# Seven block products for the first feed-forward product, an earlier second compression, and low parts on VectorE

## The chip, the cores and the metric

The kernel runs on one core of a Trainium2 chip. The metric is the device time of one launch in microseconds (us), lower is better. One profiled execution of the kernel before, with its trace, is what the prediction is made from.

## The reference, cut to what matters

One inference step of a decoder layer for 512 prompt tokens and 64 sample tokens (8 sequences of 8), which share the weights. Input projection, a sparse attention with a compressed, a selected and a window branch, a gated mixer, an output projection, and a feed-forward block:

```python
kc = compress_blocks(kv_full[:, :, 0], ...)   # keys
vc = compress_blocks(kv_full[:, :, 1], ...)   # values
h = x + jnp.concatenate([o_a, o_b], axis=-1) @ w_out
f = jax.nn.relu(rmsnorm(h, ln2_g) @ w_ff1)    # 1024 -> 4096
y = rmsnorm(h + (f * f) @ w_ff2, ln_f_g)      # 4096 -> 1024
```

## The kernel before, in words

Every large product is made in split form: an operand is cut into a high part (rounded copy, made by ScalarE) and a low part (the rest, a subtraction, mostly on VectorE), by `split` (L105). A product is then three matmuls: high with high, high with low, low with high. A weight tile of 128 rows by 512 columns is loaded into a `raw` tile and split into a unit `wu` of two halves by `load_unit` (L134).

The kernel is written in a tile framework: the author names pools of slots, the framework places every wait and, by a simulated timeline, the order of each engine's queue, with what is traced first going first among what is ready. Tiles of one tag in a pool share its slots (`bufs`).

**Sample attention** (L756 to L929) goes over four pairs of sequences. For a pair, `hidden` (L781) makes 32 matmuls `pcs` into a slot of the two-slot PSUM pool `psaA` and a `gelu` on ScalarE and VectorE; `compress_keys` (L791) follows it with a product `pk` in a slot of the same pool, `compress_values` (L798) with `pv`. Before, the tracing order for the first pair is keys' hidden, `pk`, the softmax (`soft`, L809), then values' hidden, `pv`. In `soft`, VectorE scales 1,032 columns of P and GpSimd 512 (L874).

**Output projection** (L942 to L1007). The mixer output `OTp` is split into `Hh` and `Hl` in eight pieces, the low parts on GpSimd (L995), the sample rows into `Hst`. 16 weight units `us` lie in the slots `fw` (3 + 5) and `fw2` (6 + 2). Ten groups of matmuls, one for a token tile t (four of 128 rows, t = 4 the 64 sample rows) and a column half, go in the order of L1003, sample rows last; a finished t is normed and transposed into Hh, Hl (L148).

**Feed-forward** (L1042 to L1099): eight chunks c of 512 hidden columns. `up` (L1047) makes, for each of four blocks m of 128 columns and each half of the 576 tokens (288), 24 matmuls: 192 in a chunk. `square` (L1054) makes relu, square and split into Fh, Fl; GpSimd copies the sample rows into Fst. `down` (L1072) makes ten groups: eight (t < 4) of 12 matmuls of 512 columns and two (t = 4) of 8, 112 in a chunk. `acc` (L966) adds a group onto the residual R: VectorE for t < 4; for t = 4 ScalarE copies half of it to `atmp`, VectorE adds into `atm2`, GpSimd adds onto R. `atmp` and `atm2` are tags of the pool `evp`, two slots each. PSUM for all groups are six banks taken in a fixed cycle from pools of 3, 2 and 1 (L957).

In the last chunk each t is followed by `last_norm` (L1015): ScalarE squares R into a tile `y` (tag `y`, two slots) with a row sum, VectorE and GpSimd make the factor, VectorE writes `y`, SyncE stores it. The last t (t = 3) has tiles of its own, two halves `yh`.

Of the kernel before, what the change touches and what calls it, by code (L numbers as in the profile page):

```python
# [90 lines left out]
def _body(ctx, tc, nc, I, O):  # L91
# [664 lines left out]
    with cs as c3:  # L756
# [34 lines left out]
        def compress_keys(pr, KW):  # L791
            gel = hidden(pr, 0)
            pk = psaA.tile([128, 512], F32, name="pk2", tag="acc")
# [4 lines left out]
        def compress_values(pr):  # L798
            gel = hidden(pr, 1)
            pv = psaA.tile([64, 2, 2, 64], F32, name="pv2", tag="acc")  # L800
            for sq in range(2):
                for h in range(2):
                    f = sq == 0 and h == 0
                    mm(pv[:, sq, h, :], gel[:, (h * 2 + sq) * 64:(h * 2 + sq) * 64 + 64], w2z[:, 1, 64:128],
                       f, True, f)
            dve.tensor_tensor(VB[pr][0:64].rearrange("p s (h d) -> p (s h) d", h=2),
                              pv.rearrange("p s h d -> p (s h) d"), bcast(b2r[0:64, 1], [[0, 4], [1, 64]]), op=ALU.add)
# [106 lines left out]
                        dst = OTs[gp * 64:gp * 64 + 64, h * 2 + a, c0:c0 + 16].rearrange("p (s q) -> p s q", s=2)  # L914
                        cpy("D" if h else "A", dst, ov[h * 64:h * 64 + 64, :, h, a, gp, :])

        compress_keys(0, W[0])
        prev = None
        for pr in range(4):
            P = soft(pr, W[0])  # L920
            compress_values(pr)
            if prev:
                values(*prev)
            prev = (pr, P, W[1])
            if pr < 3:
# [71 lines left out]
    split(Hst[:, :, 0:64], Hst[:, :, 64:128], OTs)  # L997
    for t in range(5):
        sp.dma_start(R[t], xin[t])
    with ExitStack() as c3:  # L1000
        n2 = c3.enter_context(tc.tile_pool(name="n2b", bufs=2, reuse_waits="tile"))
        done = set()
        for t, nh in ((0, 0), (1, 0), (2, 0), (3, 0), (0, 1), (1, 1), (2, 1), (3, 1), (4, 0), (4, 1)):  # L1003
# [7 lines left out]
    KC = 4  # L1011
    yo = [O["yp"].rearrange("b s d -> (b s) d")[t * 128:(t + 1) * 128] for t in range(4)]
    yo.append(O["ys"].rearrange("b s d -> (b s) d"))

    def last_norm(t, final):  # L1015
        rows = tsz[t]
        if final:

            y = [rp.tile([128, 512], F32, name="yh", tag=f"yh{h}", bufs=1) for h in range(2)]
            q = rp.tile([128, 512], F32, name="yq", tag="yq", bufs=1)  # L1020
            s2 = rp.tile([128, 2], F32, name="ss2", tag="ss2", bufs=1)
            ss = rp.tile([128, 1], F32, name="ssf", tag="ssf")
            for h in range(2):
                x = R[t][:, h * 512:h * 512 + 512]
                act.activation(q[:rows], x, AF.Square, accum_out=s2[:rows, h:h + 1])
                (dve if h else pool).tensor_tensor(y[h][:rows], x, gf[:rows, h * 512:h * 512 + 512], op=ALU.mult)
            dve.tensor_tensor(ss[:rows], s2[:rows, 0:1], s2[:rows, 1:2], op=ALU.add)
# [12 lines left out]

    w_ff1, w_ff2 = I["w_ff1"][0], I["w_ff2"][0]
    for c in range(32 // KC):  # L1042
        us = [load_unit(fw[k], w_ff1[k * 128:(k + 1) * 128, c * 512:c * 512 + 512], 512) for k in range(8)]
        Fh = fp.tile([128, KC, NT], F32R, name="Fh", tag="Fh")
        Fl = fp.tile([128, KC, NT], F32R, name="Fl", tag="Fl")
        Fst = fp.tile([128, KC, 128], F32R, name="Fst", tag="Fst")
# [5 lines left out]
                    mm(p[:, :288], w, a[:, k, c0:c0 + 288], k == 0 and j == 0, k == 7 and j == 2)  # L1052

        def square(m, pab):  # L1054
            r = rp.tile([128, NT], F32, name="relu", tag="relu")
            f2 = rp.tile([128, NT], F32, name="f2", tag="f2")
            for i, p in enumerate(pab):
                act.activation(r[:, i * 288:i * 288 + 288], p[:, :288], AF.Relu)  # L1058
            dve.tensor_tensor(f2, r, r, op=ALU.mult)  # L1059
            split(Fh[:, m], Fl[:, m], f2)  # L1060
            pool.tensor_copy(Fst[:, m, 0:64], Fh[:, m, 512:576].bitcast(F32))  # L1061
            pool.tensor_copy(Fst[:, m, 64:128], Fl[:, m, 512:576].bitcast(F32))

        for m0 in range(0, KC, 2):
# [7 lines left out]
        def down(t, nh, vs):  # L1072
            p = bank()
# [9 lines left out]
            acc(t, p, nh * 512, evp)  # L1083

        def down_units(nh):
            return [load_unit(fw2[nh * KC + m], w_ff2[(c * KC + m) * 128:(c * KC + m + 1) * 128, nh * 512:nh * 512 + 512], 512)
                    for m in range(KC)]

        if c < 32 // KC - 1:
# [76 lines left out]
```

## Time and profile before

| what | value |
|---|---|
| median of 3 runs | 828.01 us (827.09 to 829.6) |
| the profiled execution's own time | 827.65 us |
| its span, first to last instruction | 825.9 us |
| TensorE busy with matmuls | 789.6 us of the span |
| VectorE, ScalarE, GpSimd busy | 442.7, 353.4, 176.7 us |
| mean granted TensorE clock | 0.987 |

A row of the timeline has the start in us from the span's start, the duration, engine, line, operation, output<-inputs, shapes, a count where like instructions are merged, and in brackets the idle time of the engine just before and what ended it. PE is TensorE's matmul side, PEld its weight loads, DVE VectorE, ACT ScalarE, POOL GpSimd, SP SyncE's queue of transfers. Matmuls are pipelined, so the distance between starts is the pace, not the duration of one.

### The profile page before, as it was taken

How to read it: one execution, taken by the hardware profiler on the slowest of the kernel's cores; microseconds unless marked ns; L12 is line 12 of the kernel's file. 1: busy time of each engine (PE TensorE's matmuls, PEld its weight loads, DVE VectorE, ACT ScalarE, POOL GpSimd, SP SyncE). 2: the span in 40 equal slices, each digit the busy share in tenths (PEclk: the TensorE clock that was granted, in tenths of full speed). 3: DMA queues.
4: the chain of work that ended last, by engine and by line, in shares of the span. 5: the costliest groups of instructions: out<-in, count | busy, mean ns of one | idle time of the engine just before them, and what ended most of it. 6: DMA issues, size and time to landing. Idle time of an engine off the chain costs nothing.

```text
span 825.9 us, 13167 instructions
## 1 busy us (share of the span) xinstructions
PE 789.6 (96%) x4825; PEld 685.8 (83%) x4825; DVE 442.7 (54%) x980; ACT 353.4 (43%) x864; POOL 176.7 (21%) x219
## 2 busy tenths in 40 slices
PE   6989999999997998999989999999999999999996
PEld 5879888878675776778888998989989899898985
DVE  5345878888962347443756345163452634435325
ACT  6535478787842243432634232232322324232213
POOL 1103744454310116010211111111111111111112
PEclk9999999999997999999999999999999999999999
DMA  9771422000967545533324132041320413303003
GB/s 317 201 207 30 135 54 52 2 2 27 327 234 264 194 118 195 194 120 115 121 85 150 54 102 75 29 153 52 102 88 16 154 52 102 102 15 100 2 1 115
DMA packets 55187, 92.05 MB, mean 111 GB/s; under 512 B 7858, under 2 KB 19090, under 8 KB 54994
## 3 DMA queue, kind: packets, MB, share of 16 engines
q1 hardware_dynamic: 54866, 91.14, 34.8%
q8 instruction: 38, 0.62, 0.3%
q14 instruction: 27, 0.22, 0.1%
q0 software_dynamic: 256, 0.07, 0.0%
HBM read 86.92 MB, written 8.39 MB: 115 GB/s over the span
## 4 chain that ended last, share of the span: by engine, by line
PE 83%; DVE 7%; DMA 3%; ACT 3%; issue 2%; POOL 1%; POOLq 0%; SPq 0%; DVEq 0%; ACTq 0%
PE acc L95 52%; PE pcs L95 6%; PE pd L95 5%; PE o L95 4%; PE pu L95 3%; PE pq L95 3%; PE s L95 2%; PE tp L692 2%; DMA raw<-in_w_in 2%; DVE wu L107 1%; PE pc L95 1%; POOL wu L107 1%; DVE Q L522 1%; POOL rstd L145 1%; DMA raw<-in_w_ff 1%
## 5 line engine op out<-in xcount | busy, mean ns | idle before, releaser
L95 PE MATMUL acc<-Hh,wu 128*128 128x288 f32 x1024 | 204.9, 295 | 0.2 <-ACT Hh L106 0.2
L106 ACT ACTIVATE wu<-raw 128x512 fp32r<-128x512 f32 (+1 forms) x184 | 105.5, 614 | 152.6 <-PE acc L95 119.5
L95 PEld LDWEIGHTS acc<-Hh,wu 128*128 128x128 f32 x1024 | 164.3, 188 | 0.7 <-ACT Hh L106 0.4
L95 PE MATMUL acc<-wu,Fh 128*128 128x512 f32 x512 | 155.5, 389 | 0.0
L95 PE MATMUL acc<-Hl,wu 128*128 128x288 f32 x512 | 150.7, 295 | 0.0
L107 DVE TENSOR_TENSOR wu<-raw,wu 128x512 fp32r<-128x512 f32 x160 | 105.2, 695 | 47.2 <-ACT wu L106 47.2
L95 PEld LDWEIGHTS acc<-wu,Fh 128*128 128x128 f32 x512 | 95.7, 188 | 19.5
L95 PE MATMUL acc<-wu,Fl 128*128 128x512 f32 x256 | 97.1, 389 | 0.0
L95 PEld LDWEIGHTS acc<-Hl,wu 128*128 128x128 f32 x512 | 96.0, 188 | 0.3
L1059 DVE TENSOR_TENSOR f<-relu 128x576 f32<-128x576 f32 x32 | 24.2, 756 | 117.9 <-ACT relu L1058 117.9
L968 DVE TENSOR_TENSOR OTp<-acc,OTp 128x512 f32<-128x512 f32 x72 | 47.7, 687 | 62.4 <-PE acc L95 62.4
L1058 ACT ACTIVATE relu<-acc 128x288 f32<-128x288 f32 x64 | 26.2, 409 | 116.9 <-PE acc L95 116.9
L974 POOL TENSOR_TENSOR R<-atm,R 64x512 f32<-64x512 f32 x18 | 30.5, 1700 | 155.1 <-DVE atm L973 155.1
L95 PE MATMUL pd<-wu,AH 128*128 128x512 f32 (+1 forms) x192 | 55.2, 371 | 8.7 <-ACT wu L106 8.2
L95 PE MATMUL pcs<-G,w 128*128 128x256 f32 x256 | 61.5, 396 | 0.0
L1061 POOL CAST Fst<-Fh 128x64 fp32r<-128x64 f32 x32 | 23.5, 734 | 175.2 <-ACT Fh L106 118.7
L95 PEld LDWEIGHTS pcs<-G,w 128*128 128x128 f32 x256 | 49.7, 199 | 10.5 <-issue 3.6
L95 PEld LDWEIGHTS acc<-wu,Fl 128*128 128x128 f32 x256 | 48.1, 188 | 10.0
L95 PEld LDWEIGHTS pd<-wu,AH 128*128 128x128 f32 x192 | 34.7, 193 | 14.8 <-ACT wu L106 8.6
L668 ACT ACTIVATE P<-s,nm 128x32 f32<-128x32 f32 (+4 forms) x88 | 40.5, 464 | 14.5 <-DVE nm L667 14.0
L95 PE MATMUL acc<-wu,Hh 128*128 128x512 f32 x128 | 40.6, 397 | 0.0
L107 POOL TENSOR_TENSOR wu<-raw,wu 128x512 fp32r<-128x512 f32 (+1 forms) x24 | 30.8, 1301 | 44.2 <-ACT wu L106 44.2
(329 smaller groups left out, 1349.5 us busy)
## 6 DMA issues: line engine op xcount, KB each, us to landing
raw<-in_w_ff SPq DMA_DIRECT2D x128, 256.0 KB
G<-in_cache_kv SPq DMA_DIRECT2D x64, 256.0 KB
raw<-in_w_in SPq DMA_DIRECT2D x32, 256.0 KB
raw<-in_w_out SPq DMA_DIRECT2D x16, 256.0 KB
out_wins<-in_state_win_kv SPq DMA_DIRECT2D x8, 504.0 KB
xt<-in_x_t SPq DMA_DIRECT2D x8, 288.0 KB
x<-in_x_prompt SPq DMA_DIRECT2D x4, 512.0 KB
KW<-in_win_kt SPq DMA_DIRECT2D x4, 512.0 KB
```

The source lines that it names most:

```text
L95: pe.matmul(out, lhsT, rhs, start=start, stop=stop, skip_group_check=not first_in_bank)
L106: act.activation(hi, src, AF.Copy)
L107: eng.tensor_tensor(lo, src, hi.bitcast(F32), op=ALU.subtract)
L145: pool.tensor_tensor(r[:rows], ms[:rows], mhalf[:rows], op=ALU.pow)
L522: dve.tensor_tensor(Q[b, h, c0:c1], src, Q[a, h, c0:c1].bitcast(F32), op=ALU.subtract)
L668: act.activation(p_[:, c0:c0 + w], src, AF.Exp, bias=nm[:, br, g:g + 1], accum_out=l[:, br, g:g + 1])
L692: pe.transpose(t_[:w, g * 128:(g + 1) * 128], P[g][:, c0:c0 + w], ident)
L968: dve.tensor_tensor(R[t][:, c0:c0 + 512], p, R[t][:, c0:c0 + 512], op=ALU.add)
L974: pool.tensor_tensor(R[4][:, c0:c0 + 512], tm2, R[4][:, c0:c0 + 512], op=ALU.add)
L1058: act.activation(r[:, i * 288:i * 288 + 288], p[:, :288], AF.Relu)
L1059: dve.tensor_tensor(f2, r, r, op=ALU.mult)
L1061: pool.tensor_copy(Fst[:, m, 0:64], Fh[:, m, 512:576].bitcast(F32))
```

## The change

1. Sample attention: the first pair's two `hidden` are traced together ahead of the first `pk`; the gelu pool gets a second slot, and this first `pk` lies in the bank of `psm`.
2. The low parts of L995 go to VectorE.
3. From chunk 1 on, `up` is replaced by `seven(m0)` for each pair of blocks: the pair's product (1024 rows by 256 columns, by 576 tokens) is taken as 2 x 2 blocks of 512 rows, 128 columns and 288 tokens, and made of seven block products of 12 matmuls in place of eight. Sums of token blocks (`token_sums`, once, in chunk 0) and of weight blocks (`weight_sums`, for each pair) are made and split; the results are combined by five VectorE additions.
4. To make room: `y` has one slot, which the last t uses too; `evp` has one slot for each tag, and the weight sum `s3` and the last `yq` share the tag `atmp`; `raw` has 6 slots, `fw2` 4 + 2, the units go round two rings, `Hst` and `g2` lie in the norm pool, and sample rows come fifth in the output projection.
5. The last t's second half of `down` is made in two pieces of 256 columns.

```diff
-        ga_ = lpool("agel", 1)
+        ga_ = lpool("agel", 2)
...
-        compress_keys(0, W[0])
+        gel = [hidden(0, st) for st in range(2)]
+        compress_keys(0, W[0], gel[0], psm)
...
-            compress_values(pr)
+            compress_values(pr, gel[1] if pr == 0 else None)
...
-    pools['wraw'] = tpool("wraw2", 7)
-    evp = tpool("evp", 2)
+    pools['wraw'] = tpool("wraw2", 6)
+    evp = tpool("evp", 1)
...
-    fw2a = tpool("fw2a", 6)
-    fw2 = [fw2a] * 6 + [fw2b] * 2
+    fw2a = tpool("fw2a", 4)
+    fw2 = [fw2a] * 4 + [fw2b] * 2
...
+    ring, ring2 = itertools.cycle(fw), itertools.cycle(fw2)
...
-        split(Hh[:, k, 0:512], Hl[:, k, 0:512], OTp[:, k], pool)
-    us.append(out_units(1, fw2))
+        split(Hh[:, k, 0:512], Hl[:, k, 0:512], OTp[:, k])
+    us.append(out_units(1, fw2 + fw[:2]))
...
+    def token_sums(k):
...
+        def sub2(b, a):
+            x, y = tmp("tx"), tmp("ty")
+            dve.tensor_tensor(x, q(Hh, *b), q(Hh, *a), op=ALU.subtract)
+            dve.tensor_tensor(y, q(Hl, *b), q(Hl, *a), op=ALU.subtract)
+            dve.tensor_tensor(x, x, y, op=ALU.add)
+            return x
+        def sub1(b, x):
+            z = tmp("tz")
+            dve.tensor_tensor(z, q(Hh, *b), x, op=ALU.subtract)
+            dve.tensor_tensor(z, z, q(Hl, *b), op=ALU.add)
+            return z
+        t1 = sub2((0, 1), (0, 0))
+        split(T[0][0][:, k], T[0][1][:, k], t1)
+        t2 = sub1((1, 1), t1)
+        split(T[1][0][:, k], T[1][1][:, k], t2)
+        t4 = sub1((1, 0), t2)
+        split(T[2][0][:, k], T[2][1][:, k], t4)
+        t3 = sub2((1, 1), (0, 1))
+        split(Hh[:, k, N2:NT], Hl[:, k, N2:NT], t3)
+    def weight_sums(m0):
+        for i in range(2):
+            r = rp.tile([128, 4, 256], F32, name="fraw", tag=f"fraw{i}", bufs=1)
...
+        us = [next(ring).tile([128, 2, 512], F32R, name="wu", tag="w") for i in range(7)]
...
+        s3 = evp.tile([128, 512], F32, name="s3", tag="atmp").rearrange("p (k m) -> p k m", k=4)
+        put(0, a11)
+        dve.tensor_tensor(s3, a11, a21, op=ALU.subtract)
+        dve.tensor_tensor(a21, a21, a22, op=ALU.add)
+        dve.tensor_tensor(a11, a21, a11, op=ALU.subtract)
+        put(1, a11)
+        put(2, s3)
+        put(3, a21)
+        put(4, a12)
+        dve.tensor_tensor(a12, a12, a11, op=ALU.subtract)
+        put(5, a22)
+        put(6, a12)
+        return us
...
+            y = rp.tile([128, D], F32, name="y", tag="y", bufs=1)
...
-        y = rp.tile([128, D], F32, name="y", tag="y")
+        y = rp.tile([128, D], F32, name="y", tag="y", bufs=1)
...
+            prod(a, 0, half(H, 0, 0))
+            p1 = fs("p1")
+            act.activation(p1, a, AF.Copy)
+            prod(b, 1, T[1])
+            u = fs("u2")
+            dve.tensor_tensor(u, b, p1, op=ALU.add)
+            prod(cc, 2, half(H, 0, 1))
+            v = fs("v")
+            dve.tensor_tensor(v, cc, u, op=ALU.add)
+            prod(d, 3, T[0])
+            dve.tensor_tensor(v, d, v, op=ALU.add)
+            out(v, 1, 1)
+            prod(a, 4, half(H, 1, 0), True)
...
+            prod(cc, 5, T[2], True)
...
+            prod(d, 6, half(H, 1, 1), True)
...
         for m0 in range(0, KC, 2):
+            if c:
+                seven(m0)
+                continue
...
+        if c == 0:
+            for k in range(4):
+                token_sums(k)
```

All tiles of 288 columns (`fs`, the relu of chunk 0 and the temporaries of `token_sums` among them) are one tag with six slots.

## Rows read from the trace of the kernel before

**Rows 1.** The chain of waits, whole run: start, us, what; its longest piece.
```profile
421.01 386.70 PE acc L95 x2312
```

**Rows 2.** Windows of one chunk: up stage, down stage.
```profile
core 0: us, PE busy (x) PEld busy (x) DVE busy (x) ACT busy (x) POOL busy (x), PEclk, DMA share, GB/s
462.50:487.97 25.47, 25.47 (x194) 25.47 (x193) 8.22 (x14) 8.40 (x17) 4.08 (x6) 1.00 0.14 43
487.97:513.34 25.37, 25.37 (x113) 20.98 (x113) 14.02 (x22) 7.26 (x15) 3.40 (x5) 1.00 0.39 124
```

**Rows 3.** Timelines of VectorE and TensorE, two tiles of one PSUM tag.
```profile
55.74 1.23 DVE L456 TENSOR_TENSOR wsr<-wsr,cst 128x1024 f32<-128x1024 f32 x1
...
85.17 0.41 PE L95 MATMUL pvc<-w2z,gout 128*32 128x64 f32 x4
85.52 1.09 PE L461 MATMUL pws<-cst,wsr 128*128 128x128 f32 x8
```

**Rows 4.** Timelines of ScalarE and VectorE about the end of chunk 0.
```profile
462.92 0.58 ACT L971 ACTIVATE atmp<-acc 64x512 f32<-64x512 f32 x1
...
465.91 0.41 ACT L1058 ACTIVATE relu<-acc 128x288 f32<-128x288 f32 x1 [1.90 <-PE acc L95]
...
462.00 1.90 DVE L107 TENSOR_TENSOR wu<-raw,wu 128x512 fp32r<-128x512 f32 x3 [0.42 <-ACT wu L106]
...
472.66 0.76 DVE L1059 TENSOR_TENSOR f<-relu 128x576 f32<-128x576 f32 x1 [7.57 <-ACT relu L1058]
```

**Rows 5.** Timeline of TensorE, first pair of the sample attention.
```profile
234.82 4.48 PE L95 MATMUL pcs<-G,w 128*128 128x256 f32 x20
...
246.93 1.09 PE L95 MATMUL o<-ptf,Vc 32*128 32x512 f32 x2 [1.66 <-DVE OTp L711]
...
253.61 1.23 PE L95 MATMUL pk<-gsq,w2z 128*128 128x128 f32 x4 [3.39 <-DVE gsq L1126]
254.63 6.62 PE L95 MATMUL pcs<-G,w 128*128 128x256 f32 x20
...
268.88 0.68 PE L95 MATMUL pv<-w2z,gsq 128*64 128x64 f32 x8 [1.27 <-DVE gsq L1126]
```

**Rows 6.** Timelines of GpSimd and VectorE, sample attention.
```profile
317.86 12.05 POOL L107 TENSOR_TENSOR Hl<-OTp,Hh 128x512 fp32r<-128x512 f32 x8 [16.86 <-PE o L95]
...
298.77 0.89 DVE L103 TENSOR_SCALAR P<-P,r 128x8 f32<-128x8 f32 x2
...
324.56 2.96 DVE L103 TENSOR_SCALAR P<-P,r 128x8 f32<-128x8 f32 x2
...
339.06 0.23 DVE L829 TENSOR_REDUCE nm<-w_a 128x1 f32<-128x64 f32 x1 [7.83 <-PE w_a L95]
```

**Rows 7.** Timeline of TensorE, start of the feed-forward.
```profile
420.11 0.68 PE L159 MATMUL ptr<-cst,xn 64*128 64x64 f32 x8 [1.87 <-DVE xn L154]
```

**Rows 8.** Timelines of ScalarE and GpSimd, tail.
```profile
806.23 1.06 ACT L1036 ACTIVATE y<-R 64x1024 f32<-64x1024 f32 x1 [3.53 <-POOL R L974]
821.74 0.72 ACT L1029 ACTIVATE yh<-yh,rstd 128x512 f32<-128x512 f32 x1 [1.11 <-POOL rstd L145]
...
816.83 1.30 POOL L1026 TENSOR_TENSOR yh<-OTp,gf 128x512 f32<-128x512 f32 x1
```

**Rows 9.** The chain of waits: a load, and the tail.
```profile
407.30 5.02 DMA raw<-in_w_ff
...
809.64 0.02 SPq L1039
...
812.74 1.16 ACT y L1036 x2
...
815.98 0.03 issue
```

**Rows 10.** Windows of 10 us, sample attention to feed-forward, columns as above.
```profile
250.00:260.00 10.00, 6.61 (x20) 5.37 (x20) 1.98 (x5) 2.22 (x5) 0.00 (x0) 0.55 0.66 215
...
410.00:420.00 10.00, 8.24 (x64) 8.01 (x62) 9.24 (x13) 5.31 (x11) 4.30 (x3) 1.00 0.72 234
```

More of the change, by code (lines that the diff above doesn't have):

```diff
@@ L789, in hidden, with compress_keys @@
             return gelu(nc, ga_, pc[:, 1:257], 256, b1p[:, st, 0:1], b1p[:, st, 1:2], out="sq")
-        def compress_keys(pr, KW):
-            gel = hidden(pr, 0)
-            pk = psaA.tile([128, 512], F32, name="pk2", tag="acc")
+        def compress_keys(pr, KW, gel=None, bank=None):
+            gel = gel or hidden(pr, 0)
+            pk = (bank or psaA).tile([128, 512], F32, name="pk2", tag="mm" if bank else "acc")
             mm(pk[:, :128], w2z[:, 0, 64:192], gel[:, 0:128], True, False)
@@ L796, in compress_keys, with compress_values @@
             act.activation(KW[:, :, 0:64], pk[:, :128].rearrange("p (s n) -> p s n", s=2), AF.Identity, bias=b2c[:, 0:1])
-        def compress_values(pr):
-            gel = hidden(pr, 1)
+        def compress_values(pr, gel=None):
+            gel = gel or hidden(pr, 1)
             pv = psaA.tile([64, 2, 2, 64], F32, name="pv2", tag="acc")
@@ L1001, in _body @@
         n2 = c3.enter_context(tc.tile_pool(name="n2b", bufs=2, reuse_waits="tile"))
+        Hst = n2.tile([128, 8, 128], F32R, name="Hst", bufs=1)
+        g2 = bload(n2, I["ln2_g"], D, "g2")
+        split(Hst[:, :, 0:64], Hst[:, :, 64:128], OTs)
         done = set()
-        for t, nh in ((0, 0), (1, 0), (2, 0), (3, 0), (0, 1), (1, 1), (2, 1), (3, 1), (4, 0), (4, 1)):
+        for t, nh in ((0, 0), (1, 0), (2, 0), (3, 0), (4, 0), (0, 1), (1, 1), (2, 1), (3, 1), (4, 1)):
             out_proj(t, nh, us[nh])
@@ L1011, in _body, with q, tmp @@
     KC = 4
+    N2 = NT // 2
+    tp_ = ctx.enter_context(tc.tile_pool(name="tsum", bufs=1))
+    T = [[tp_.tile([128, 4, N2], F32R, name=f"T{i}{j}") for j in "hl"] for i in (1, 2, 4)]
+    def token_sums(k):
+        def q(a, i, j):
+            return a[:, 4 * i + k, j * N2:j * N2 + N2].bitcast(F32)
+        def tmp(name):
+            return rp.tile([128, N2], F32, name=name, tag="fs", bufs=6)
+        def sub2(b, a):
[17 more added lines that the diff above has]
+        split(Hh[:, k, N2:NT], Hl[:, k, N2:NT], t3)
@@ new lines, in weight_sums, with put @@
+    def weight_sums(m0):
+        raw = []
+        for i in range(2):
+            r = rp.tile([128, 4, 256], F32, name="fraw", tag=f"fraw{i}", bufs=1)
+            sp.dma_start(r, w_ff1[i * 512:i * 512 + 512, m0 * 128:m0 * 128 + 256].rearrange("(k p) m -> p k m", p=128))
+            raw.append(r)
+        us = [next(ring).tile([128, 2, 512], F32R, name="wu", tag="w") for i in range(7)]
+        def put(i, src):
+            v = us[i].rearrange("p s (k m) -> p s k m", k=4)
+            split(v[:, 0], v[:, 1], src)
+        (a11, a21), (a12, a22) = ([raw[i][:, :, m * 128:m * 128 + 128] for m in range(2)] for i in range(2))
+        s3 = evp.tile([128, 512], F32, name="s3", tag="atmp").rearrange("p (k m) -> p k m", k=4)
[11 more added lines that the diff above has]
+        return us
@@ L1017, in last_norm @@
         if final:
-            y = [rp.tile([128, 512], F32, name="yh", tag=f"yh{h}", bufs=1) for h in range(2)]
-            q = rp.tile([128, 512], F32, name="yq", tag="yq", bufs=1)
-            s2 = rp.tile([128, 2], F32, name="ss2", tag="ss2", bufs=1)
+            y = rp.tile([128, D], F32, name="y", tag="y", bufs=1)
+            y = [y[:, h * 512:h * 512 + 512] for h in range(2)]
+            q = evp.tile([128, 512], F32, name="yq", tag="atmp")
+            s2 = rp.tile([128, 3], F32, name="ss2", tag="ss2", bufs=1)
             ss = rp.tile([128, 1], F32, name="ssf", tag="ssf")
[L1023 to L1027, printed above, removed]
+            for i, (c0, n) in enumerate(((0, 512), (512, 256), (768, 256))):
+                x = R[t][:, c0:c0 + n]
+                act.activation(q[:rows, :n], x, AF.Square, accum_out=s2[:rows, i:i + 1])
+                (dve if i else pool).tensor_tensor(y[i > 0][:rows, c0 % 512:c0 % 512 + n], x, gf[:rows, c0:c0 + n], op=ALU.mult)
+            dve.tensor_reduce(ss[:rows], s2[:rows], axis=AX, op=ALU.add)
             r = rstd_of(rp, ss, D, rows)
@@ L1042, in _body @@
     for c in range(32 // KC):
-        us = [load_unit(fw[k], w_ff1[k * 128:(k + 1) * 128, c * 512:c * 512 + 512], 512) for k in range(8)]
+        if c == 0:
+            us = [load_unit(next(ring), w_ff1[k * 128:(k + 1) * 128, c * 512:c * 512 + 512], 512) for k in range(8)]
         Fh = fp.tile([128, KC, NT], F32R, name="Fh", tag="Fh")
@@ L1054, in square @@
         def square(m, pab):
-            r = rp.tile([128, NT], F32, name="relu", tag="relu")
-            f2 = rp.tile([128, NT], F32, name="f2", tag="f2")
             for i, p in enumerate(pab):
-                act.activation(r[:, i * 288:i * 288 + 288], p[:, :288], AF.Relu)
-            dve.tensor_tensor(f2, r, r, op=ALU.mult)
-            split(Fh[:, m], Fl[:, m], f2)
+                r = rp.tile([128, N2], F32, name="relu", tag="fs", bufs=6)
+                act.activation(r, p[:, :N2], AF.Relu)
@@ L1061, in square, with stack, seven, half @@
+                dve.tensor_tensor(r, r, r, op=ALU.mult)
+                sl = slice(i * N2, i * N2 + N2)
+                split(Fh[:, m, sl], Fl[:, m, sl], r)
+            stack(m)
+        def stack(m):
             pool.tensor_copy(Fst[:, m, 0:64], Fh[:, m, 512:576].bitcast(F32))
             pool.tensor_copy(Fst[:, m, 64:128], Fl[:, m, 512:576].bitcast(F32))
+        def seven(m):
+            us = weight_sums(c * KC + m)
+            a, b, cc, d = (bank()[:, :N2] for i in range(4))
+            def half(x, i, j):
+                return [y[:, 4 * i:4 * i + 4, j * N2:j * N2 + N2] for y in x]
+            H = (Hh, Hl)
+            def prod(p, i, x, more=False):
+                for k in range(4):
+                    wh, wl = (us[i][:, s, k * 128:k * 128 + 128] for s in range(2))
+                    for j, (w, y) in enumerate(((wh, x[0]), (wh, x[1]), (wl, x[0]))):
+                        mm(p, w, y[:, k], not more and k == 0 and j == 0, k == 3 and j == 2, not more)
+            def fs(name):
+                return rp.tile([128, N2], F32, name=name, tag="fs", bufs=6)
+            def out(x, i, j, square=True):
+                if square:
+                    act.activation(x, x, AF.Relu)
+                act.activation(x, x, AF.Square)
+                sl = slice(j * N2, j * N2 + N2)
+                split(Fh[:, m + i, sl], Fl[:, m + i, sl], x)
+            prod(a, 0, half(H, 0, 0))
[11 more added lines that the diff above has]
+            prod(a, 4, half(H, 1, 0), True)
+            r = fs("c11")
+            act.activation(r, a, AF.Relu)
+            out(r, 0, 0, False)
+            prod(cc, 5, T[2], True)
+            w = fs("c21")
+            dve.tensor_tensor(w, cc, u, op=ALU.add)
+            out(w, 1, 0)
+            stack(m + 1)
+            prod(d, 6, half(H, 1, 1), True)
+            w = fs("c12")
+            dve.tensor_tensor(w, d, u, op=ALU.add)
+            out(w, 0, 1)
+            stack(m)
@@ L1070, in _body, with down @@
                 square(m0 + m, pab[m])
-        def down(t, nh, vs):
-            p = bank()
+        if c == 0:
+            for k in range(4):
+                token_sums(k)
+        def down(t, nh, vs, c0=0, n=512):
+            p = bank()[:, :n]
+            vs = [v[:, :, c0:c0 + n] for v in vs]
             for m in range(KC):
@@ L1096, in _body @@
             for t in (4, 0, 1, 2, 3):
-                for nh in range(2):
-                    down(t, nh, vs[nh])
+                down(t, 0, vs[0])
+                for c0, n in (((0, 256), (256, 256)) if t == 3 else ((0, 512),)):
+                    down(t, 1, vs[1], c0, n)
                 last_norm(t, t == 3)
```

10 lines of the change are left out of this document (4 added, 6 removed).

## Prediction

> **What bounds the kernel now.** I read the chain of waits first: its longest piece is one unbroken run of matmuls from 421.01 for 386.70 us, the whole feed-forward [rows 1]. So there only TensorE's pace, or a wait put into that run, moves the end; elsewhere VectorE and ScalarE have slack. The windows of one chunk give the pace: 25.47 us for 192 matmuls of 288 columns in the up stage (0.1327 each), 25.37 for 112 in the down stage, at a granted clock of 1.00 (its upper level, 2.4 GHz) [rows 2]. VectorE is busy 8.22 and 14.02 us in them. Then the timelines: where TensorE stands idle ahead of the feed-forward [rows 5, 7], what follows one another in the tail [rows 8, 9], and how two tiles of one tag are served [rows 3]. That view decides most of what follows: `wsr` was ready at 56.97 (55.74 + 1.23), yet its transposes run at 85.52, straight behind those of `pvc`, traced earlier with the same PSUM tag. A later tile of a tag does not pass an earlier one. The change cuts tags to one slot, so that order now binds in three places.
>
> **Block products, the gain.** Chunks 1 to 7 have two pairs each, 14. A pair goes from 8 x 12 to 7 x 12 matmuls: 14 x 12 x 0.1327 = 22.3 us less. One block product lasts 12 x 0.1327 = 1.59. All of it lies on the path [rows 1, 2], so −22.3. The row's 0.1327 us is the pace of matmuls that each load weights of their own. The Trainium skill, page TensorE: Matmul & The Clock Gate, section Back-to-back issue gap, gives the isolated gap as N/2.4 + 2.5 ns, 122.5 ns for 288 columns; as an estimate from that page the term would be −20.6. The measured pace is kept.
>
> **Wait at a chunk's start.** The weight sum `s3` of a chunk's first pair shares the only slot of the tag `atmp` with the sample rows' last group of the chunk before, traced earlier and run as the last group of the down stage. So `s3` comes after ScalarE's copy into `atmp` and VectorE's addition that reads it, and the sums behind `s3` follow on VectorE, each overwriting what the one before has read. From the end of that group: ScalarE starts 0.23 after a group's last matmul (the first group of a chunk ends at 462.50 + 24 x 0.1327 = 465.68, its relu starts at 465.91) and copies 0.58; VectorE starts one addition of 512 columns each 0.61 (three in 1.90, the last 0.07 longer), and four are wanted (`atm2`, `s3`, `a21`, `a11`), 2.51; then a high part of about 0.58, a low part of 0.68 (0.61 + 0.07), and three handovers of 0.05: 4.7 us to the third matmul of the second block product [rows 4]. TensorE has meanwhile the first product, 1.59, and two matmuls, 0.27, so it stands 2.9. A product whose sum is ready one step (0.61) sooner can be taken first, 2.3; between them I take 2.4. In chunks 3 and 7 the ring's position lets the parts of untouched blocks be made ahead, and I keep half, 1.2. 5 x 2.4 + 2 x 1.2 = **+14.4**. Bounds: 0, if the slot comes free in time; 28, if every pair of the seven chunks stands 2 us (14 x 2).
>
> **Second pair of a chunk.** Its `fraw` tiles have one slot, so their transfer starts only when the first pair's sums are read. The trace has a store of 3.10 (812.74 less 809.64) and a load of 5.02 [rows 9]; five more block products, some 8 us, cover either. At nothing; if that cover went, up to 5.02 − 3.10 = 1.9 us a chunk (a rival).
>
> **Chunk 0.** `token_sums` is 56 subtractions and additions of 288 columns on VectorE. The row has 0.76 for 576 columns [rows 4], half of it 0.38: 21.3 us. With ten additions of the down stage and three split steps at 0.61 that is 29 us in a stage of 25.4 [rows 2]. These are also served in order behind chunk 0's relus, which lie in the same six slots. **+3.5**, between 0 (the surplus runs on under chunk 1) and 8.
>
> **First pair's compression.** TensorE idles 1.66, 3.39 and 1.27 about it, 6.3, and right behind the longest gap 20 matmuls take 6.62 where the same 20 took 4.48 before, 2.1 more [rows 5], with the clock at 0.55 [rows 10], so mostly at its lower level, 1.2 GHz. With both `hidden` traced ahead of `pk`, values' 32 matmuls move into the stretch that the prompt rows' attention fills. Of 8.4 I leave the 1.66, which ends on VectorE's `OTp`, not on a gelu: **−6.7**, between 0 and −8.4. No transfer moves: the weights of both are loaded before.
>
> **Low parts on VectorE.** GpSimd's eight took 12.05 us, and inside them VectorE's scaling of P took 2.96 where it takes 0.89 [rows 6]. That stretching goes, 2.1 on this step and some 1 on its neighbours: **−3.0**. The eight now cost VectorE 8 x 0.61 = 4.9, under its idle of 7.83 [rows 6]; without that cover +2, so −4 to +2.
>
> **Start of the feed-forward.** The sample rows come fifth, so their norm no longer ends the stage: the idle of 1.87 [rows 7] goes. But two of the units of the second half now lie in ring slots that chunk 0 wants, whose second and third units start only when the last output group has read them: 0.23 + 0.58 + 0.68 [rows 4] is 1.4 or so. **−0.5**, between −1.9 and +2.
>
> **Tail.** All five last norms share one slot of `y`. A norm's Square can start only when the store before has landed. From Square to written `y` is 3.24 (812.74 to 815.98), from there to the next Square 3.10 (809.64 to 812.74): a link of 6.34 [rows 9], against 5.4 us of matmuls for a token tile (24 x 25.37 / 112). The first Square came at 806.23 [rows 8]; one slot of `atm2` makes it about 1.0 later. Four links bring 832.6; then GpSimd's multiplication 1.30, ScalarE's scaling 0.72 with 0.2 of handovers, and the last store 3.44 (the span's end, 825.9, less 822.46) [rows 8]: 838.2 against 825.9, **+12.3**, 11 to 14. The two pieces of 256 columns shorten a path that no longer ends last: nothing.
>
> **Sum:** −22.3 + 14.4 + 3.5 − 6.7 − 3.0 − 0.5 + 12.3 = −2.3. The profiled execution's 827.65 becomes 825.35; the median of the runs stood 0.36 above it, so **825.7**. With the terms' bounds this case reaches from 820 to 833.
>
> **Rivals.**
> - *The chunk-start wait does not bite*: the sums are placed ahead of the copy, or another product fills the time. For it: TensorE has six more block products of which some need only untouched blocks. Against it: [rows 3]. Without 14.4 it is 811.3, faster. Chance 0.25.
> - *The second pair stands too* (slower): the `fraw` load, issued late behind the down units on SyncE's queue, takes 5.02 and not 3.10, and the ring passes no unit ahead. It decides once the load lands over 8 us after the first pair's sums. 7 x 1.9 = +13.3, 839.0. Against it: transfers use only 0.14 of their time in the up stage [rows 2]. Chance 0.10.
> - *The clock falls after each chunk-start wait* (slower): behind the idle of 3.39 the clock stood at 0.55 [rows 5, 10]; 7 x 2.1 = +14.7, 840.4. Against it: after 1.87 idle [rows 7], around 418, the window's clock stayed at 1.00 [rows 10]. Chance 0.10. The Trainium skill's same page, section Part 1: The HAM clock gate, sets the clock by how busy TensorE has lately been; by that rule the waits could cost twice, and the two rows bear it out for the longer idle alone.
> - *The first pair's gain does not come*, the change not doing there what it says, since `pk` and the gelus still queue on VectorE in the old order: 832.4. Chance 0.10 (slower 0.07, same 0.03).
> - The forecast itself: 0.45.
>
> **How the numbers follow.** A measurement of this kernel can tell 0.3%, 2.5 us, from no change, so the same is 825.5 to 830.5. My case lies at its lower edge: of its 0.45, faster 0.20, same 0.18, slower 0.07. With the rivals: faster 0.20 + 0.25 = 0.45, same 0.18 + 0.03 = 0.21, slower 0.07 + 0.07 + 0.10 + 0.10 = 0.34. The range takes in 811.3 less 3 for the other bounds, and 841 above.
>
> **What would show it.** Up stages of about 22.3 us and, behind each chunk's first product, a gap of about 2.4 on TensorE that ends on `wu` from ScalarE or VectorE; at the tail ScalarE's `y` waiting for the store each time, and a span that ends some 20 us after the last matmul; the 64 `pcs` of the first pair close together at 1.00 clock; the scaling of P at 0.89; VectorE near full in chunk 0's down stage. No gap at the chunk starts, or a last store no later behind the last matmul than before, would make the prediction wrong.

## The result, and the profile after

The changed kernel takes 892.54 us (median of 4 runs, 890.54 to 893.87) against 827.85 before: a ratio of 1.0769, 95% interval [1.0741, 1.0797]. It is slower by 65 us. The forecast was 825.7, in a range of 808 to 841, which does not contain the result. The profiled execution has a span of 890.0 against 825.9, so 64.1 us are to be found in it.

Three stretches, cut at TensorE's own rows. From the first matmul of the first pair's `hidden` to the end of chunk 0: 227.83 before (234.82 to 462.65), 238.04 after (233.03 to 471.07), and the stretch ahead of it is 1.8 shorter: +8.4 together. From there to the last matmul: 355.9 before, 387.2 after, +31.3. Behind the last matmul: 7.3 before, 31.7 after, +24.4. The sum is 64.1. In the timeline of TensorE of the kernel before, the last matmul is this row, which ends at 818.58:

```profile
818.19 0.39 PE L95 MATMUL acc<-wu,Fl 128*128 128x512 f32 x1
```

**The seven chunks.** Windows of the changed kernel, chunks 1 to 7, each from the end of the chunk before; the columns are those of [rows 2], the last line their sum.

```profile
471.07:532.43 61.36, 51.37 (x280) 46.15 (x280) 38.85 (x74) 26.37 (x57) 15.44 (x10) 0.89 0.22 69
532.43:586.54 54.11, 51.07 (x282) 45.83 (x280) 35.02 (x61) 25.04 (x53) 7.77 (x10) 0.94 0.25 78
586.54:639.69 53.15, 50.31 (x282) 44.96 (x281) 32.68 (x57) 22.49 (x49) 7.28 (x10) 0.97 0.26 80
639.69:695.07 55.38, 50.81 (x281) 46.13 (x280) 34.13 (x59) 23.63 (x51) 7.19 (x10) 0.94 0.25 76
695.07:751.20 56.13, 50.98 (x282) 45.79 (x280) 33.42 (x59) 23.63 (x51) 7.65 (x10) 0.94 0.24 75
751.20:804.77 53.57, 48.76 (x282) 43.39 (x281) 34.93 (x61) 25.11 (x53) 8.49 (x10) 1.00 0.26 80
804.77:858.30 53.53, 50.78 (x293) 45.53 (x291) 30.22 (x54) 21.29 (x46) 8.05 (x11) 0.97 0.06 20
sum 387.23, PE 354.08 PEld 317.79 DVE 239.25 ACT 167.55 POOL 61.86; mean PE 50.58 PEld 45.40 DVE 34.18 ACT 23.94 POOL 8.84
```

A chunk has 280 matmuls in place of 304, yet takes 53 to 61 us in place of 50.84 [rows 2]. TensorE is idle for 387.23 − 354.08 = 33.2 us, 10.0 of them in chunk 1; and six of the seven chunks show a granted clock under 1.00. The gap at a chunk's start, on the chain of waits about the start of chunk 2:

```profile
532.54 0.94 DVE wu L107 x2
...
533.75 0.67 DVE atm L975
...
534.95 0.69 DVE s L1067
...
535.66 1.64 DVE fraw L1068
537.30 0.60 DVE wu L107
537.90 0.60 DVE fraw L1069
538.51 1.81 DVE wu L107 x3
...
542.33 4.73 DMA fraw<-in_w_ff
```

`s` (the tile `s3` of the program) stands behind `atm`, the addition that frees the shared slot; the sums follow on VectorE; and the second pair's load leaves only when its slots have been read, and ends on the chain too. TensorE meanwhile (timeline, then windows of the 8 us from the end of the longer gap on):

```profile
536.34 0.61 PE L95 MATMUL acc<-Hh,wu 128*128 128x288 f32 x1 [2.17 <-ACT wu L106]
...
537.96 0.85 PE L95 MATMUL acc<-Hh,wu 128*128 128x288 f32 x2 [0.77 <-DVE wu L107]
```

```profile
536.43:540.43 4.00, 3.23 (x12) 2.88 (x13) 4.00 (x7) 2.30 (x4) 0.32 (x1) 0.50 0.22 75
540.43:544.43 4.00, 4.00 (x23) 4.00 (x22) 1.78 (x3) 0.63 (x1) 0.00 (x0) 0.68 0.48 145
```

Behind the gap the clock stands at 0.50, the lower of its two levels.

At the second pair TensorE shows no gap in this chunk, though the load is on the chain. It has such gaps in three chunks: 1.10 us in chunk 1, 0.78 in chunk 5, and 1.04 and 0.50 in chunk 6, 3.4 in all. The longest of chunk 6, in the timeline of TensorE:

```profile
764.14 0.40 PE L95 MATMUL acc<-Hh,wu 128*128 128x288 f32 x1 [1.04 <-ACT wu L106]
```

**The tail.** Timelines of TensorE (the sample rows' last group, in three pieces) and of ScalarE:

```profile
850.96 0.39 PE L95 MATMUL acc<-wu,Fst 128*128 128x512 f32 x1
851.98 0.63 PE L95 MATMUL acc<-wu,Fst 128*128 128x512 f32 x2
854.85 0.40 PE L95 MATMUL acc<-wu,Fst 128*128 128x512 f32 x1
```

```profile
858.42 1.06 ACT L1104 ACTIVATE y<-R 64x1024 f32<-64x1024 f32 x1 [0.64 <-POOL R L976]
...
864.74 1.06 ACT L1104 ACTIVATE y<-OTp 128x1024 f32<-128x1024 f32 x1 [4.23 <-DMA out_ys<-y]
...
870.79 1.06 ACT L1104 ACTIVATE y<-OTp 128x1024 f32<-128x1024 f32 x1 [4.90 <-DMA out_yp<-y]
...
876.89 1.06 ACT L1104 ACTIVATE y<-OTp 128x1024 f32<-128x1024 f32 x1 [4.96 <-DMA out_yp<-y]
```

The chain of norms and stores is there, with links of 6.05 to 6.32. But its first Square comes at 858.42, at the last matmul, where before it came 12.4 us ahead of it [rows 8]: the sample rows, first in the last chunk, finish only at 855.

**Ahead of the feed-forward.** Timelines of ScalarE (units being split; other rows left out) and of TensorE in the last pair:

```profile
339.96 0.63 ACT L106 ACTIVATE wu<-raw 128x512 fp32r<-128x512 f32 x1 [3.25 <-PE o L95]
347.21 0.63 ACT L106 ACTIVATE wu<-raw 128x512 fp32r<-128x512 f32 x1 [2.65 <-DMA raw<-in_w_out]
...
355.77 0.63 ACT L106 ACTIVATE wu<-raw 128x512 fp32r<-128x512 f32 x1 [3.84 <-DMA raw<-in_w_out]
359.90 0.63 ACT L106 ACTIVATE wu<-raw 128x512 fp32r<-128x512 f32 x1 [3.50 <-DMA raw<-in_w_out]
```

```profile
353.96 0.31 PE L883 MATMUL tp<-cst,P 128*80 128x128 f32 x1 [1.46 <-DVE P L103]
...
357.50 1.12 PE L888 MATMUL tp<-cst,P 128*128 128x128 f32 x4 [2.56 <-DVE PTn L884]
...
361.16 1.09 PE L888 MATMUL tp<-cst,P 128*128 128x128 f32 x4 [1.92 <-ACT PT L99]
```

Output matmuls filled these gaps before. Now only a part of each sum can be made, because units four to eight are not there; and the units that are split come one at a time, each behind its own load, some 4 us apart. From the first `hidden` to the end of chunk 0 TensorE is idle for 20.5 us in place of 13.9, and busy for 217.6 in place of 213.9: the clock is at 0.78 from 344 to 367 and at 0.82 from 414.56 to 424, where the kernel before shows 1.00 from 344 on.

### The profile page after: what moved, and what is told of

The parts are those of the page before. It is cut to its first block, busy times and chain, and to the rows that moved or that the text cites. A ratio compares the mean times of both kernels' runs of the same rounds, so it can differ in the third digit from the quotient of the medians.

```text
span 890.0 us, 13105 instructions
## 1 busy us (share of the span) xinstructions
PE 790.7 (89%) x4669; PEld 680.0 (76%) x4669; DVE 545.1 (61%) x1222; ACT 418.2 (47%) x1026; POOL 172.5 (19%) x211
## 4 chain that ended last, share of the span: by engine, by line
PE 69%; DVE 15%; DMA 7%; ACT 4%; issue 3%; POOL 1%; DVEq 0%; SPq 0%; ACTq 0%; POOLq 0%
PE acc L95 40%; PE pcs L95 7%; PE pd L95 5%; PE o L95 4%; DVE wu L107 4%; PE pu L95 3%; PE pq L95 3%; DMA fraw<-in_w_ff 3%; PE s L95 2%; PE tp L692 2%; ACT wu L106 2%; DMA raw<-in_w_in 2%; DMA raw<-in_w_out 1%; DVE fraw L1068 1%; DMA out_yp<-y 1%
## 5 line engine op out<-in xcount | busy, mean ns | idle before, releaser
L95 PE MATMUL acc<-wu,Fh 128*128 128x512 f32 (+1 forms) x520 | 157.7, 386 | 0.0
L95 PE MATMUL acc<-Hh,wu 128*128 128x288 f32 x576 | 133.0, 312 | 24.5 <-ACT wu L106 18.1
L95 PEld LDWEIGHTS acc<-Hh,wu 128*128 128x128 f32 x576 | 101.4, 200 | 29.5 <-ACT wu L106 19.9
L970 DVE TENSOR_TENSOR OTp<-acc,OTp 128x512 f32<-128x512 f32 (+1 forms) x73 | 49.1, 680 | 82.4 <-PE acc L95 82.4
L95 PE MATMUL acc<-wu,Fl 128*128 128x512 f32 (+1 forms) x260 | 99.0, 386 | 0.0
L95 PE MATMUL acc<-Hl,wu 128*128 128x288 f32 x288 | 88.8, 309 | 0.0
L107 DVE TENSOR_TENSOR wu<-raw,wu 128x512 fp32r<-128x512 f32 x104 | 69.4, 697 | 29.1 <-ACT wu L106 29.1
L106 ACT ACTIVATE wu<-fraw 128x512 fp32r<-128x512 f32 x84 | 50.1, 623 | 68.5 <-DMA fraw<-in_w_ff 42.6
L107 DVE TENSOR_TENSOR wu<-fraw,wu 128x512 fp32r<-128x512 f32 x84 | 55.7, 683 | 8.4 <-ACT wu L106 8.0
L95 PEld LDWEIGHTS acc<-Hl,wu 128*128 128x128 f32 x288 | 58.0, 202 | 0.5
L107 POOL TENSOR_TENSOR wu<-raw,wu 128x512 fp32r<-128x512 f32 (+1 forms) x24 | 30.8, 1301 | 43.4 <-ACT wu L106 43.4
```

Of the source, the lines that this page charges most:

```text
L95: pe.matmul(out, lhsT, rhs, start=start, stop=stop, skip_group_check=not first_in_bank)
L106: act.activation(hi, src, AF.Copy)
L107: eng.tensor_tensor(lo, src, hi.bitcast(F32), op=ALU.subtract)
L970: dve.tensor_tensor(r, p, r, op=ALU.add)
```

## The experiments

Differences in us are ratios, or differences of ratios, times 828.

### The shared slot of the weight sum

```diff
-        s3 = evp.tile([128, 512], F32, name="s3", tag="atmp").rearrange(...
+        s3 = rp.tile([128, D], F32, name="y", tag="y", bufs=1)[:, :512].rearrange(...
```

> The changed kernel with the weight sum `s3` in the slot of `y`, free until the tail, in place of the slot shared with `atmp`. Theory A (the chunk-start gap and the lower clock behind it come from that shared slot): in chunks 2 to 7 the gaps of 2.2 to 4.6 us go, the clock stays at 1.00, and 6 chunks lose some 2.5 of gap and 2.8 of clock each: 892.5 falls by 20 to 37 us, to 855 to 872. Rival B (the second pair's load or VectorE's backlog ends last there anyway): less than 8 us, over 884.

847.02 us, ratio 1.0229 [1.0167, 1.0291]: 45 us less than the change, more than theory A's own range. Windows of chunks 1 to 3:

```profile
469.25:525.82 56.57, 52.83 (x283) 46.05 (x282) 44.99 (x91) 27.74 (x61) 15.06 (x10) 0.94 0.21 66
525.82:573.54 47.72, 47.72 (x282) 43.30 (x282) 33.58 (x60) 23.30 (x51) 7.41 (x10) 1.00 0.28 89
573.54:621.26 47.72, 47.72 (x282) 43.30 (x282) 33.67 (x60) 23.32 (x51) 7.38 (x10) 1.00 0.28 89
```

From chunk 2 on there is no gap, the clock stays at 1.00, and no second pair waits for its load: all three came from the one slot. A chunk takes 47.72, and 50.84 − 47.72 = 3.12 is the measured worth of two saved block products. Chunk 1 still takes 8.9 more; VectorE is busy for 45 of its 56.6 us.

### Eight products, all else as changed

```diff
-            if c:
-                seven(m0)
-                continue
...
-        if c == 0:
-            us = [load_unit(next(ring), w_ff1...
+        if True:
+            us = [load_unit(next(ring), w_ff1...
...
-        if c == 0:
-            for k in range(4):
-                token_sums(k)
```

> The changed kernel with eight block products in every chunk, no token sums and no weight sums; all else as changed (first pair, low parts, pools, rings, one slot of `y`). Theory A (the seven chunks lose their time to the sums' waits and the clock alone): chunks take 50.84 us again without a gap, so 31 us go from chunks 1 to 7 and 0 to 4 from chunk 0, 892.5 becomes 856 to 862, with front and tail as in the changed kernel. Rival B (the smaller pools of `raw` and of the down units stop TensorE in every chunk too): over 868.

861.95 us, ratio 1.0395 [1.0337, 1.0453], as theory A has it: chunks of 50.85 without a gap. So with eight products fewer slots for `raw` and for the down units stop nothing in chunks 1 to 6. The tail is still 30.8 us (span 859.7, last matmul until 828.9), and the front still long: 32 to 33 us of the loss have nothing to do with the seven products.

### The tail: slots of the down units, then of y

```diff
-            return [load_unit(next(ring2), w_ff2[(c * KC + m)...
+            return [load_unit(next(ring if c == 7 and nh and m > 1 else ring2), w_ff2[(c * KC + m)...
```

> The changed kernel with the last two of the last chunk's eight down units in slots of the eight-slot ring of the up stage, so that eight slots serve eight units. Theory A (the sample rows' second half waits for slots that the first halves of all token tiles hold, so all last norms start at the end): the sample rows' Square starts some 12 us ahead of the last matmul as before the change, the end moves from 32 us behind the last matmul to 20, and the time falls by 10 to 14 us, to 879 to 883. Rival B (the one slot of `y` alone makes the tail): no change.

881.66 us, ratio 1.0652 [1.059, 1.0714], 10 us less than the change. Timeline of ScalarE (last matmul until 855.9):

```profile
845.00 1.07 ACT L1104 ACTIVATE y<-R 64x1024 f32<-64x1024 f32 x1 [2.79 <-POOL R L976]
...
851.73 1.06 ACT L1104 ACTIVATE y<-OTp 128x1024 f32<-128x1024 f32 x1 [5.57 <-DMA out_ys<-y]
```

The first Square is 10.9 us ahead of the last matmul's end again, and the tail is 20.8, the size that the prediction gave it. The last chunk needs eight down units at once, since each token tile goes through both halves; the changed ring has six slots, so units seven and eight waited until units one and two had served all first halves, the last token tile's included.

The second run adds a place for each `y`, in the memory of the token sums, which nothing reads after the last up stage:

```diff
+    def y_of(t):
+        tag = ("T1h", "T1l", "T4h", "T4l", "T2h")[t]
+        return tp_.tile([128, 4, N2], F32, name="y", tag=tag).rearrange("p k n -> p (k n)")[:, :D]
...
-        y = rp.tile([128, D], F32, name="y", tag="y", bufs=1)
+        y = y_of(t)
```

> The changed kernel with eight slots for the last chunk's down units and a place of its own for each `y`. Theory A (behind the units' slots, the chain of norm and store over the one slot of `y` is what makes the rest of the tail): the last store lands 7 to 9 us behind the last matmul, and 881.7 falls by 11 to 14 us, to 868 to 871. Rival B (the norms are late for the engines' queues): less than 6 us.

868.54 us, ratio 1.047 [1.0427, 1.0513], 15 us less again (the medians differ by 13), as theory A has it. The tail is 8.5 us (span 866.5, last matmul until 858.0). In the timeline of ScalarE the first three Squares now follow one another without a store between:

```profile
847.36 1.06 ACT L1108 ACTIVATE y<-R 64x1024 f32<-64x1024 f32 x1 [2.78 <-POOL R L976]
...
848.42 1.04 ACT L1108 ACTIVATE y<-OTp 128x1024 f32<-128x1024 f32 x1
...
849.46 1.04 ACT L1108 ACTIVATE y<-OTp 128x1024 f32<-128x1024 f32 x1
```

### The place of the five units

```diff
-    fwb = tpool("fwb", 5)
-    fw = [fwa] * 3 + [fwb] * 5
     fw2a = tpool("fw2a", 4)
+    fwb = tpool("fwb", 5)
+    fw = [fwa] * 3 + [fwb] * 5
```

> The changed kernel with the pools of the five units `fwb` and the four units `fw2a` in swapped order of allocation, so that the five lie where the third pair's pages were, as before the change, and the four where the last pair's window tiles are. Theory A (output units four to eight of the changed kernel cannot be made until the last pair's window keys and values have been read, since their memory overlaps): the output projection's second half of each sum begins near 345 and not near 367, the idle of TensorE between 352 and 367 goes, and the time falls by 6 to 12 us, to 880 to 887. Rival B (the serial loads come from six `raw` slots in place of seven): no change, 890 to 895.

892.24 us, ratio 1.0765 [1.0698, 1.0833]: in the time, nothing, and theory A's range is missed. Its mechanism is in the timeline of ScalarE all the same:

```profile
342.01 2.71 ACT L106 ACTIVATE wu<-raw 128x512 fp32r<-128x512 f32 x5 [3.24 <-PE o L95]
```

All five are split at once; the changed kernel splits the same five from 366.92 on. There are six `raw` slots as there, so the serial loads are not a matter of six slots alone; the rows fit five of the six having held loaded parts of units that had no place. From the first `hidden` to the end of chunk 0 this execution takes 232.88 us (236.08 to 468.96) against 238.04. But it reached 236.08 three us later than the changed kernel's reached 233.03, and the stretch ahead of that point differs by up to 4.6 us between executions of these kernels, whose code there is the same. The gain of 5 is shown in one execution's stretch; in the total it is inside the spread.

### Two parts of the change alone, on the kernel before

Part 1 (first pair's `hidden` together, second gelu slot, `pk` in the other bank), as in the change's diff; then the low parts of the mixer output:

> The kernel before with part 1 of the change alone: the first pair's two compressions traced together, second slot for the gelu, first `pk` in the other bank. Theory A (what the prediction put at -6.7, by the changed kernel's trace, where the second pair's `pk` starts 6.0 us earlier than before): faster by 3 to 7 us, 821 to 825. Rival B (the output projection's first matmuls filled the time anyway, so that an earlier second pair is given back there): within 2 us of the kernel before.

826.76 us, ratio 0.9967 [0.9941, 0.9992]: 2.7 us faster. From the first `hidden` to the second pair's `pk` it takes 40.5 us where it took 44.5, so 4.0 are gained there. But the first pair's longest gap stays (timeline of TensorE):

```profile
259.62 1.20 PE L95 MATMUL pk<-gsq,w2z 128*128 128x128 f32 x4 [3.64 <-DVE gsq L1127]
...
261.80 5.84 PE L95 MATMUL pcs<-G,w 128*128 128x256 f32 x16
```

The first `pk` still waits for its gelu, 3.64 where it waited 3.39, and the matmuls behind it are still slow; what is gone are the gaps of 1.66 and 1.27 [rows 5]. Of the 4.0, 2.0 are left at the third pair's `pk` (67.6 from the first `hidden`, against 69.6), and 1.9 at the last transposes ahead of chunk 0; what takes the rest was not tried. At the end of chunk 0 half a us is left in this execution (227.36 against 227.83), and that loss is the clock's. The transposes' row of this run, then windows of the 4 us from there, of this run and of the kernel before:

```profile
419.05 0.68 PE L159 MATMUL ptr<-cst,xn 64*128 64x64 f32 x8 [1.86 <-DVE xn L154]
```

```profile
419.05:423.05 4.00, 3.78 (x21) 3.64 (x22) 1.18 (x3) 1.29 (x3) 0.00 (x0) 0.58 0.08 29
```

```profile
420.11:424.11 4.00, 3.78 (x31) 3.64 (x32) 1.19 (x3) 1.29 (x3) 0.00 (x0) 1.00 0.11 38
```

Behind an idle of 1.86 the clock is at 0.58 here; behind the same idle of 1.87 [rows 7] it is at 1.00 there.

```diff
-        split(Hh[:, k, 0:512], Hl[:, k, 0:512], OTp[:, k], pool)
+        split(Hh[:, k, 0:512], Hl[:, k, 0:512], OTp[:, k])
```

> The kernel before with part 2 of the change alone: the eight low parts of the mixer output on VectorE in place of GpSimd. Theory A (the prediction's -3.0: the scaling of P is not stretched to 2.96 any more): faster by 1 to 4 us, 824 to 827. Rival B (the eight stand in VectorE's queue ahead of the last pair's steps, as in the changed kernel between 335 and 341, where TensorE then idles 0.95 and 1.82): slower by 0 to 3 us, 828 to 831.

828.68 us, ratio 0.9989 [0.9966, 1.0011], 0.9 us less, between the two theories: no difference that can be told from none. Timelines of VectorE and of TensorE show why:

```profile
318.18 4.29 DVE L107 TENSOR_TENSOR Hl<-OTp,Hh 128x512 fp32r<-128x512 f32 x7
...
328.13 0.88 DVE L103 TENSOR_SCALAR P<-P,r 128x8 f32<-128x8 f32 x2
```

```profile
329.06 0.39 PE L883 MATMUL tp<-cst,P 128*80 128x128 f32 x1 [3.09 <-DVE P L103]
```

The scaling of P is short again (0.88 against 2.96), but it starts at 328.13 where it started at 324.56 [rows 6], behind the eight low parts; TensorE waits for it 3.09 where it waited 0.97.

### GpSimd beside the weight sums

```diff
-            pool.tensor_tensor(R[4][:, c0:c0 + 512], tm2, R[4][:, c0:c0 + 512], op=ALU.add)
+            dve.tensor_tensor(R[4][:, c0:c0 + 512], tm2, R[4][:, c0:c0 + 512], op=ALU.add)
```

> The changed kernel with the sample rows' last addition onto R on VectorE in place of GpSimd. Theory A (the second weight sum takes 1.65 at each chunk's start because GpSimd's addition runs beside it): it takes 0.7 as elsewhere, the gaps at the chunk starts shrink by 0.3 to 1, and the time falls by 2 to 10 us, to 882 to 890. Rival B (1.65 is that instruction's own cost in place): it stays at 1.65, and the time is 892 to 898, with VectorE's addition in the chain.

891.47 us, ratio 1.0748 [1.0713, 1.0783]. The second weight sum, line L1068 of the changed kernel and then of this one (durations in ns: least, median, most):

```profile
L1068 DVE TENSOR_TENSOR fraw<-fraw x14: 674/693/1667, 479.1 to 819.3; 128x512 f32<-128x512 f32 x14
```

```profile
L1068 DVE TENSOR_TENSOR fraw<-fraw x14: 676/691/694, 482.2 to 818.4; 128x512 f32<-128x512 f32 x14
```

Theory A holds for the instruction: without GpSimd beside it, it never takes 1.65. Its time does not follow: the addition itself, now on VectorE, takes 0.67 in the same chain.

### The mends together

Four mends: the two pools swapped, eight slots for the last units, `s3` in a slot of its own (a tag `s3`, in the room that `y` leaves), `y_of`.

> The changed kernel with four mends together: the two pools of units swapped, eight slots for the last chunk's eight down units, `s3` in a slot of its own, and a place of its own for the `y` of each last norm (in the memory of the token sums, read for the last time in the last up stage). Theory A (the four waits are separate and their prices add up): 892.5 less 45 (`s3`), 11 (units of the tail), 12 (stores of the tail) and 0 to 5 (pools swapped): 819 to 825, faster than before. Rival B (the prices overlap, or the stretch ahead of the feed-forward ends later by other waits): 828 or more.

823.74 us, ratio 0.9929 [0.9903, 0.9955]: 0.7% under the kernel before, 5.9 us, and inside the range of theory A, so the prices add up. What is left in chunk 1, 57.1 us, led to the next two. They trace the first three of the four token sums for all four k, then for two of them, right behind chunk 0's first two blocks:

```diff
             for m in range(2):
                 square(m0 + m, pab[m])
+            if m0 == 0:
+                for k in range(2):
+                    token_sums(k, 0)
...
-                token_sums(k)
+                for part in ((1,) if k < 2 else (0, 1)):
+                    token_sums(k, part)
```

> The kernel with four mends, and the token sums cut in two: three of the four sums of each k are traced behind chunk 0's first two blocks, in VectorE's slacker up stage, and only the fourth, which overwrites a part of Hh and Hl, stays behind chunk 0's up stage. Theory A (what chunk 1 still loses in the kernel with four mends, 57.1 us from chunk 0's last group to its own against 47.7 in chunk 2, is VectorE's backlog of token sums): chunk 1 takes 48 to 52 us, and 823.7 falls by 4 to 9 us, to 815 to 820. Rival B (the temporaries, served in one order with the relus from the same six slots, hold up chunk 0's up stage instead): within 3 us of 823.7 or slower, with new gaps in chunk 0.

820.14 us, ratio 0.9894 [0.9872, 0.9916]. Chunk 1 now takes 47.72 as the others do, which is theory A; but the time falls by 3 us where it said 4 to 9, and rival B is right too, in the timeline of TensorE in chunk 0:

```profile
456.22 1.22 PE L95 MATMUL acc<-wu,Fh 128*128 128x512 f32 x2 [8.28 <-ACT relu L1132]
```

The second blocks' relus stood behind the token sums' temporaries.

> The kernel with four mends and early token sums, but early for two of the four k alone; the other two stay behind chunk 0's up stage. Theory A (the gap of 8.3 us that the early sums left in chunk 0 is VectorE's queue ahead of the second blocks' relus and squares, some 4 us for two k): the gap is 0 to 4 us, chunk 1 takes 48 to 52, and the time lies 2 to 6 us under that with all four early, 814 to 818. Rival B (the six slots, not VectorE's time, hold the relus, so any early sum costs the whole gap): a gap of 6 to 9 again and 820 or more.

815.69 us, ratio 0.9846 [0.9818, 0.9873], 12 to 13 us faster than the kernel before. The gap of 8.28 is gone; chunk 1 takes 51.1 us, with two gaps of 0.84 and 1.12.

## Why the prediction was wrong

Stretch by stretch, the forecast had −22.3 + 14.4 = −7.9 for the seven chunks, and they took +31.3; it had 12.3 for the tail, and it took 24.4; it had −6.7 for all that lies ahead, and it took +8.4. The steps that failed most are the wait at a chunk's start (the wait too short, and the clock left out of it) and the tail (a wait for unit slots left out).

**Block products, −22.3: right.** Measured 7 x 3.12 = 21.8 in undisturbed chunks. The estimate from the Trainium skill, page TensorE: Matmul & The Clock Gate, section Back-to-back issue gap, −20.6, is 1.2 off where the row of this kernel is 0.5 off.

**Wait at a chunk's start, +14.4: the right place, and the size wrong.** The slot chain is what the runs show: give `s3` another slot, and 45 us go. The step put a gap of 1.2 to 2.4 into each of the seven chunks. Measured in chunks 2 to 7 are 23.2 us idle, 20.8 of them at the first pair, 3.5 a chunk. In chunk 2 the chain was longer by the stretch of the second weight sum beside GpSimd's addition (about 1.0) and by a low part of another weight unit between `atm` and `s` (0.6), and a second gap came behind the first. In chunk 1, 10.0 more, part of it VectorE's token sums.

**Two rivals were not rivals.** The second pair's late load (0.10) and the falling clock (0.10) were set beside the forecast, each with a price of its own. They hang on the forecast's wait: the gap delays the sums, so the slots of `fraw`, so the load; and behind the gap the clock can fall. With the wait given, both came, the load with 3.4 us (+13.3 was its price), the clock with about 354.08 − 7 x 47.72 = 20 us of TensorE's busy time (+14.7 was its price). This is the step that failed most in chunks 1 to 7: the forecast's own case should have carried the clock's 14.7 and some of the 13.3 beside its 14.4. The row held against the clock's fall, 1.00 [rows 10], is of a window that ended at 420.00, just ahead of the end of the idle of 1.87 [rows 7]. The 4 us behind that idle show 1.00 too, but with part 1 alone the same idle was followed by 0.58: one row could not settle it. The Trainium skill, page TensorE: Matmul & The Clock Gate, section Part 1: The HAM clock gate, sets the clock by how busy TensorE has lately been; the row at 0.50 behind the first gap agrees, the one at 1.00 in chunk 6 (below) behind a gap as long does not show it.

**Chunk 0, +3.5: in the wrong chunk.** From 424 to the end of chunk 0 TensorE is never idle, with VectorE busy for 23.97 of the last 25.07 us. The surplus ran on under chunk 1, which the step had priced at nothing; there 8.9 us were left with `s3` mended. They left chunk 1 when the sums were traced earlier, in part into chunk 0.

**Tail, +12.3: half.** The chain over `y` was right: links near 6.1 (forecast 6.34), and with eight unit slots a tail of 20.8, 13.5 more than before; a place for each `y` took 12.3 of that away. What failed is that `fw2` with six slots was passed over: the last chunk wants eight units at once, which its own loop shows (both halves are taken ahead of the first token tile). That is another 10 to 11 us.

**First pair, −6.7: −2.7 (interval −4.9 to −0.7).** The step took the gap of 3.39 ahead of `pk` and the slow matmuls behind it to go, and left the 1.66 standing. With part 1 alone it is the other way: `pk` still waits 3.64, and the 1.66 is gone.

**Low parts, −3.0: −0.9, not to be told from nothing.** The scaling of P became short as said, but the cover of 7.83 us lay behind it, while VectorE took the eight low parts ahead of it.

**Start of the feed-forward, −0.5.** Only the first half of the sample rows' columns comes fifth; the second still goes last (`(4, 1)` in the change's order), so their norm still ends the stage, against what the step and the part on the change say. The idle of 1.87 went, and 1.84 for `Hh`, behind five splits on ScalarE, came in its place, with 0.56 and 0.80 behind it. And the step looked for what waits on the two moved units alone. Making pools smaller also moved every pool behind them, and put the five units `fwb` where the last pair's window tiles are still read: 5 us in the trace. How the rest of the 10.2 us between the first `hidden` and the end of chunk 0 divides was not tried; 6.6 of them are idle time, 3.6 busy time, with the clock lower in the two stretches named above.

## What to carry to other kernels

When tags are cut to one slot, count for each the tiles alive at once, and follow the last reader: a slot shared by work at the end of one stage and the start of the next is a wait at every border. A rival that needs the forecast's own wait to happen is a term of the sum, not a rival. A single row of the clock behind a gap of about 2 us does not say what the next execution's will be. And after any change of a pool's size, look again at what each later pool now lies on.

## What was not expected of the hardware

The clock does not follow from the gap's length alone. With part 1 alone it was at 0.58 behind an idle of 1.86, in the kernel before at 1.00 behind 1.87. In chunk 2 it fell to 0.50 behind an idle of 2.17; in chunk 6 of the same execution it stayed at 1.00 behind the same (timeline of TensorE, then the windows about it):

```profile
755.11 0.40 PE L95 MATMUL acc<-Hh,wu 128*128 128x288 f32 x1 [2.17 <-ACT wu L106]
```

```profile
751.20:757.20 6.00, 2.73 (x18) 2.27 (x17) 5.96 (x10) 3.65 (x7) 2.25 (x1) 1.00 0.54 175
757.20:761.20 4.00, 4.00 (x32) 4.00 (x31) 3.78 (x7) 1.84 (x4) 0.00 (x0) 1.00 0.10 18
```

What decides between them stays open. The other was the stretch of the addition on VectorE from 0.69 to 1.65 beside a single addition on GpSimd of 2.27. Beside the same addition (588.61 to 590.88) two more VectorE operations of 128 x 512 took 0.68 each, unstretched; which one is stretched stays open too.
